# The opening of a decoder trunk: x loaded ahead on two queues, the norm chain ahead, and the first modulation columns as products on TensorE

## The chip, the cores and the metric

The kernel runs on one core of one Trainium2 chip, as one program. The metric is the device time of one execution in microseconds (us). Three runs of the kernel before gave 2087.95, 2089.53 and 2090.7 us, so the median is 2089.53 us. One more execution was taken with the hardware profiler on; all lines of the profile come from that one.

The engines of the core are TensorE (PE; its weight loads are listed as PEld), VectorE (DVE), ScalarE (ACT), GpSimd (POOL) and SyncE (SP). Each takes the instructions of its own queue in order. Transfers are issued by an engine's queue (here SP, and after the change ScalarE too) and run on 16 shared DMA engines.

## The reference, cut to what matters

Two layers, each of three sub-layers (SwiGLU FFN, token mixer, SwiGLU FFN), over 512 tokens of 1024 features. Every sub-layer starts with a normalised and modulated copy of x; its shift, scale and gate come from one conditioning vector c.

```
cond = silu(c)
mod = (cond @ ada_w[i] + ada_b[i]).reshape(bsz, 3, 3, D_MODEL)
shift, scl, gate = mod[:, :, 0], mod[:, :, 1], mod[:, :, 2]
h = rms_norm(x, norm_g[i, 0]) * (1 + scl[:, 0]) + shift[:, 0]
x = x + HALF * gate[:, 0] * swiglu(h, ffn_w_in[i, 0], ffn_w_out[i, 0])
```

rms_norm divides each token by the root of the mean square of its 1024 features. Nothing of the first FFN can be multiplied before the first slice of h is there, and for that the norm of x and the first scale and shift are needed.

## The kernel before, in words

x lies transposed in on-chip memory, as eight slices of 128 features by 512 tokens (`x[d]`, d from 0 to 7). All matmuls of the FFN run in three passes: each operand is split into a high part and a low part (`whi`, `wlo` for weights, `hhi`, `hlo` for h), and `mm3` (L167 to L170) multiplies high by high, high by low and low by high. ScalarE makes a high part (L164), VectorE the low part (L165).

The opening consists of these steps, and each step is traced in this order:

- The loads (L88 to L96), all on SP's queue: c broadcast to 128 partitions (`cond`, 512 KB), then the eight slices of x, with the small tables of norm gains and biases (`ngs`, `adabs`) after the fourth. ScalarE applies Silu to `cond` (L107).
- `Norm.start` (L251 to L269), the norm chain: ScalarE squares each slice (L254), VectorE adds the squares up (L256), TensorE sums over partitions with four one-column products (L260), VectorE computes the reciprocal root by integer trick and three Newton steps (L262, L195 to L203), VectorE scales the identity by it (`dg`, L267), and TensorE spreads it over all partitions with two products of 256 columns (L268).
- `ffn_first` (from L417) then walks over d. For each slice, `ada_first(d)` (L145) brings the scale and the shift of that slice: two tiles of 512 KB of modulation weights, each multiplied with `cond` and summed along the free axis. This is one VectorE instruction (L123), but the shift tile of an odd slice is multiplied on GpSimd (L120) and summed on ScalarE (L121). Three small VectorE instructions add the bias and the gain (L129, L130, L135). The tiles share a ring of four buffers (`ada`, L86), and SP issues their loads (L117).
- In the same step of d, for d below 6, one weight tile of the first FFN is loaded and split (`ffn_in`, `weights`, L172 to L180).
- `Norm.whole(d)` (L271 to L278): VectorE multiplies the slice with the norm (`xr`, L274), ScalarE applies scale and shift twice (`hhi` L275, `hf` L277), VectorE forms the low part (`hlo` L278).
- Last, TensorE multiplies what has become possible: with slice d, all weight tiles that are there. Six results (`hs`) grow side by side over the eight slices. Then the other tiles of the FFN (`gu`) follow.

The order of each engine's queue is not written by hand: a scheduler sorts the traced instructions by priority, which is the order of tracing unless a block says `tc.high_priority()`, and by the time at which it expects them to be ready.

Of the kernel before, what the change touches and what calls it, by code (L numbers as in the profile page):

```python
# [11 lines left out]
F32 = mybir.dt.float32  # L12
# [8 lines left out]
P = 128  # L21
# [20 lines left out]
NMOD = 24  # L42
NADA = 24
FIRST = 3
GC0 = math.sqrt(2.0 / math.pi)
GC1 = 0.044715
RSQ = float(0x5F3759DF)
# [1 line left out]


@with_exitstack
def decoder_kernel(ctx, tc, xT, cT, ng, adaw, adab, ffi, ffo, cwi, cw, cwo,
                   nwi, nwg, pos, w1, w2, qg, kg, nwo, rb, onehot, rowok, out):
    nc = tc.nc

# [29 lines left out]
    ada_es = ctx.enter_context(ExitStack())  # L85
    ap = ada_es.enter_context(tc.tile_pool(name="ada", bufs=4))  # L86
    cond = ap.tile([P, D], F32, name="cond", bufs=1)
    nc.sync.dma_start(cond, bass.AP(tensor=cT.tensor, offset=cT.offset, ap=[[0, P], [1, D]]))  # L88
    x = [cst.tile([P, T], F32, name=f"x{d}") for d in range(KD)]
    ngs = cst.tile([P, NSUB * KD], F32, name="ngs")  # L90
    adabs = cst.tile([P, NSUB * NMOD], F32, name="adabs")
    for d in range(KD):
        nc.sync.dma_start(x[d], xT[d])
        if d == 3:
            nc.sync.dma_start(ngs, ng)
            nc.sync.dma_start(adabs, adab)  # L96
    ident = cst.tile([P, P], F32, name="ident")
    make_identity(nc, ident)
    ones = cst.tile([P, P], F32, name="ones")
# [4 lines left out]
    rowm = cst.tile([P, 1], F32, name="rowm")  # L104
    mods = cst.tile([P, NSUB * NMOD], F32, name="mods")

    nc.scalar.activation(cond, cond, AF.Silu)  # L107

    def mod(s, kind, d):
        c = s * NMOD + kind * KD + d  # L110
# [1 line left out]

    def ada_tile(ap, s, t, split=False):
        raw = ap.tile([P, D], F32, name="adaraw")
        nc.sync.dma_start(raw, adaw[s * NADA + t])  # L117
        m = mods[:, s * NMOD + t:s * NMOD + t + 1]
        if split:
            nc.gpsimd.tensor_tensor(raw, raw, cond, ALU.mult)  # L120
            nc.scalar.activation(raw, raw, AF.Copy, accum_out=m)  # L121
        else:
            nc.vector.tensor_tensor_reduce(out=raw, in0=raw, in1=cond, scale=1.0, scalar=0.0,  # L123
                                           op0=ALU.mult, op1=ALU.add, accum_out=m)
# [12 lines left out]
    def ada_gate(s):  # L137
# [3 lines left out]
        else:  # L141
            nc.vector.tensor_add(mods[:, c:c + KD], mods[:, c:c + KD], adabs[:, c:c + KD])
            nc.vector.tensor_scalar(mods[:, c:c + KD], mods[:, c:c + KD], 0.5, None, op0=ALU.mult)

    def ada_first(ap, d):  # L145
        ada_tile(ap, 0, d)
        ada_tile(ap, 0, KD + d, d % 2 == 1)
        ada_scale(0, d, d + 1)
        ada_shift(0, d, d + 1)

    def ada_jobs(ap, s):
        lo = 2 * KD if s == 0 else 0
# [55 lines left out]
    class Norm:  # L208
# [40 lines left out]


        def start(self):  # L251
            for d in range(KD):
                dst = self.acc if d == 0 else tmp("sq", tag="sq")
                nc.scalar.activation(dst, x[d], AF.Square)  # L254
                if d:
                    nc.vector.tensor_tensor(self.acc, self.acc, dst, ALU.add)  # L256
            self.all = psum("pr", "pr")
            pv = psum("pr", "pr")
            for t in range(NB):
                nc.tensor.matmul(pv[:, t:t + 1], self.acc[:, t * P:(t + 1) * P], ones[:, 0:1], start=True, stop=True)  # L260
            v = sp.tile([P, NB], F32, name="nv", tag="nv", padded_shape=[P, NB])
            nc.vector.tensor_scalar(v, pv[:, 0:NB], 1.0 / D, EPS, op0=ALU.mult, op1=ALU.add)  # L262
            r = rsqrt(v, NB)
            for hf in range(2):
                dg = tmp("dg", HT, "dg").rearrange("p (a b) -> p a b", a=2)
                for t in range(2):
                    nc.vector.tensor_scalar(dg[:, t, :], ident, r[:, 2 * hf + t:2 * hf + t + 1], None, op0=ALU.mult)  # L267
                nc.tensor.matmul(self.all[:, hf * HT:(hf + 1) * HT], ones, dg.rearrange("p a b -> p (a b)"),  # L268
                                 start=True, stop=True)  # L269

        def whole(self, d):  # L271
            sc, sh = mod(self.s, 0, d), mod(self.s, 1, d)
# [141 lines left out]

    def ffn_first(s, f, nrm, nxt, extra, ahead, first, soon, own):  # L417
        with ExitStack() as es:
            hp = pool(es, "hp", 1)
            hid = Hidden(es, 18)  # L420
            h = nrm.alloc(hp)
            nj = FIRST
            early = spread(soon, PARTS[0][1] - nj)
            late = spread(extra, NJ - PARTS[0][1] + 2 * KD)

            def fill():
                early() if soon else late()

            js = [(j, c) for j in range(nj) for c in range(2)]
            w, os = [], [psum("hs") for _ in js]  # L430
            for d in range(KD):
                first(d)
                if d < len(js):
                    w.append(ffn_in(f, *js[d], own=own if d > 2 else None))
                nrm.whole(d)
                for n in range(len(w)):
                    for k in range(0 if n == d else d, d + 1):
                        project(os[n], w[n], 0, h, [(k, k)], k == 0, k == KD - 1)
            for j in range(nj):
                hid.activate(os[2 * j], os[2 * j + 1])  # L440
            for p, (j0, j1) in enumerate(PARTS):
                for j in range(max(j0, nj), j1):
                    hid.activate(*pair(f, j, h, own))
                    fill()
                n = j1 - j0
                a, ka = (hid.hi[j0:j1], hid.lo[j0:j1]), [(k, k) for k in range(n)]
                last = p == len(PARTS) - 1
                for d in range(KD - 3 if last else KD):
                    w = ffn_out(f, d, 1, j0, j1, own if d % 2 else None)
                    o = psum("y")  # L450
                    project(o, w, 0, a, ka, True, True)
                    if last:
                        residual(s, d, o, nxt)
# [664 lines left out]
    def ffn_ahead(f):  # L1118
# [2 lines left out]
    nxt = Norm(1)  # L1121
    soon = upto(1)
    w = ffn_first(0, 0, nrm, nxt, [small] + upto(2, NADA // 2), lambda: [weights(cwi[c], KD, P) for c in range(3)],
                  lambda d: ada_first(ap, d), soon, ap)
    nrm, nxt = nxt, Norm(2)
    w = conv(1, nrm, nxt, upto(6), w, ffn_ahead(1), ap)
    ada_es.close()
# [29 lines left out]
def _layout(v):  # L1157
    a = {k: np.asarray(t) for k, t in v.items()}
    r = {}
    r["xT"] = a["x"][0].T.reshape(KD, P, T)  # L1160
    r["cT"] = a["c"]
    r["ng"] = a["norm_g"].reshape(NSUB, KD, P).transpose(2, 0, 1).reshape(P, -1)

    cols = [(s * 3 + kind) * KD + d for s in range(3) for kind in (1, 0, 2) for d in range(KD)]
    aw = a["ada_w"].reshape(2, D, 3 * NMOD, P)[:, :, cols, :]
    r["adaw"] = aw.transpose(0, 2, 3, 1).reshape(2 * 3 * NMOD, P, D)
# [24 lines left out]
    return {k: np.ascontiguousarray(t) for k, t in r.items()}  # L1191
# [18 lines left out]
```

## Time and profile before

| | us |
|---|---|
| median of three runs | 2089.53 |
| the profiled execution, whole | 2082.89 |
| its span, from the first to the last instruction | 2081.1 |
| TensorE's first product of the first FFN (`hs`) | at 27.36 |
| first product after it (`gu`) | at 69.03 |
| TensorE busy in the span | 1985.5 |

A row of a timeline has the start in us from the span's start, the length in us, the engine, the line of the code, the operation, output and inputs by the program's names, shapes, and a count; in square brackets stands how long the engine had been idle and what ended the wait. SPq is SP's queue of transfers. A row of a group has, after the count, the busy time of the group in us, the mean of one instruction in ns, and the idle time before the group. Matmuls are pipelined, so a row's length is longer than the distance to the next row; distances between starts are used for rates.

### The profile page before, as it was taken

The numbers are of one execution on the slowest core, as the hardware profiler recorded it, in microseconds if no ns is written. First come the engines' busy times: TensorE is split into PE (matmuls) and PEld (weight loads), VectorE is DVE, ScalarE is ACT, GpSimd is POOL, SyncE is SP. The second block draws the span as 40 slices with busy tenths as digits, with TensorE's granted clock in tenths as the row PEclk, the third lists the DMA queues.
The fourth block names the chain that finished last, engine by engine and source line by source line (L and its number), as shares of the span: only waits on it lengthen the run. The fifth ranks groups of instructions, "written<-read, shape, count | busy, mean of one in ns | idle before, by whom it ended". The sixth has DMA issues, their size and how long they took to land.

```text
span 2081.1 us, 32232 instructions
## 1 busy us (share of the span) xinstructions
PE 1985.5 (95%) x12404; PEld 1769.8 (85%) x12404; DVE 1506.3 (72%) x2658; ACT 894.0 (43%) x1404; POOL 275.7 (13%) x395
## 2 busy tenths in 40 slices
PE   4999999999999999999999999988999989999999
PEld 3878888888888999888889989888788778898989
DVE  7878888664476677668767766784888868675855
ACT  4422223332254334335433433653767856343432
POOL 1000000100011111110111111000344530011100
PEclk9999999999999999999999999999999999999999
DMA  7888988322235556561455654223111133465642
GB/s 270 309 303 318 331 310 317 141 96 77 91 97 126 153 142 166 147 173 42 131 145 145 164 142 147 84 92 100 41 38 43 36 97 91 121 165 160 159 118 82
DMA packets 110662, 307.38 MB, mean 148 GB/s; under 512 B 14923, under 2 KB 15307, under 8 KB 110508
## 3 DMA queue, kind: packets, MB, share of 16 engines
q1 hardware_dynamic: 89532, 260.48, 37.1%
q0 software_dynamic: 20976, 44.84, 11.2%
q8 instruction: 97, 1.59, 0.3%
q14 instruction: 57, 0.47, 0.1%
HBM read 302.12 MB, written 3.15 MB: 147 GB/s over the span
## 4 chain that ended last, share of the span: by engine, by line
PE 38%; DVE 7%; ACT 4%; issue 2%; DMA 1%; POOL 0%; DVEq 0%; ACTq 0%; POOLq 0%; SPq 0%
PE gu L168 6%; PE gu L169 6%; PE gu L170 6%; PE y L168 4%; PE y L169 4%; PE y L170 4%; ACT whi L164 1%; DVE wlo L165 1%; DVE L L942 1%; PE nat L168 1%; PE nat L170 1%; PE nat L169 1%; PE s L932 1%; DVE ptl L977 1%; PE ty L170 1%
## 5 line engine op out<-in xcount | busy, mean ns | idle before, releaser
L164 ACT ACTIVATE whi<-wraw 128x1024 fp32r<-128x1024 f32 (+2 forms) x296 | 295.3, 1001 | 589.8 <-PE y L169 237.9
L165 DVE TENSOR_TENSOR wlo<-wraw,whi 128x1024 fp32r<-128x1024 f32 (+2 forms) x296 | 340.4, 1152 | 85.2 <-ACT whi L164 82.7
L168 PE MATMUL gu<-hhi,whi 128*128 128x256 f32 (+1 forms) x808 | 266.8, 330 | 2.0 <-ACT whi L164 2.0
L169 PE MATMUL gu<-hlo,whi 128*128 128x256 f32 (+1 forms) x808 | 266.5, 330 | 0.0
L170 PE MATMUL gu<-hhi,wlo 128*128 128x256 f32 (+1 forms) x808 | 266.1, 329 | 0.0
L168 PE MATMUL y<-ahi,whi 128*128 128x512 f32 x611 | 241.8, 399 | 3.5 <-ACT ahi L164 3.5
L169 PE MATMUL y<-alo,whi 128*128 128x512 f32 x611 | 244.4, 400 | 0.0
L170 PE MATMUL y<-ahi,wlo 128*128 128x512 f32 x611 | 241.2, 395 | 0.0
L487 POOL DMA_DIRECT2D qa<-in_ffi x114 | 103.8, 991 | 650.3 <-DMA qa<-in_ffi 335.4
L123 DVE CUSTOM_DVE_ANT_0 adaraw<-adaraw,cond 128x1024 f32<-128x1024 f32 x140 | 169.2, 1221 | 21.0 <-DMA adaraw<-in_adaw 20.0
L168 PEld LDWEIGHTS gu<-hhi,whi 128*128 128x128 f32 x808 | 152.2, 188 | 19.1 <-ACT whi L164 3.9
L169 PEld LDWEIGHTS gu<-hlo,whi 128*128 128x128 f32 x808 | 151.8, 188 | 15.5
L170 PEld LDWEIGHTS gu<-hhi,wlo 128*128 128x128 f32 x808 | 152.1, 188 | 14.9
L164 ACT ACTIVATE qbh<-qb 128x1536 fp32r<-128x1536 f32 x57 | 84.9, 1490 | 164.7 <-PE gu L169 143.5
L168 PEld LDWEIGHTS y<-ahi,whi 128*128 128x128 f32 x611 | 114.7, 189 | 36.3 <-ACT ahi L164 7.8
L554 DVE SCALAR_TENSOR_TENSOR x<-y,mods,x 128x512 f32<-128x512 f32 x72 | 54.1, 751 | 120.5 <-PE y L170 120.5
L168 PE MATMUL gu<-th,qah 128*128 128x256 f32 x456 | 131.0, 287 | 9.2 <-ACT p L512 9.2
L170 PEld LDWEIGHTS y<-ahi,wlo 128*128 128x128 f32 x611 | 115.5, 189 | 27.6
L169 PEld LDWEIGHTS y<-alo,whi 128*128 128x128 f32 x611 | 115.6, 189 | 26.3 <-DVE alo L165 0.3
L170 PE MATMUL gu<-th,qal 128*128 128x256 f32 x456 | 130.8, 287 | 0.0
L169 PE MATMUL gu<-tl,qah 128*128 128x256 f32 x456 | 130.5, 286 | 0.0
L168 PE MATMUL gu<-th,qbh 128*128 128x256 f32 x456 | 129.4, 284 | 0.0
(280 smaller groups left out, 5168.0 us busy)
## 6 DMA issues: line engine op xcount, KB each, us to landing
adaraw<-in_adaw SPq DMA_DIRECT2D x144, 512.0 KB, 5.5
wraw<-in_ffi SPq DMA_DIRECT2D x119, 512.0 KB, 4.3
qa<-in_ffi SPq DMA_DIRECT2D x114, 256.0 KB, 4.1
qa<-in_ffi POOLq DMA_DIRECT2D x114, 256.0 KB, 5.4
wraw<-in_ffo SPq DMA_DIRECT2D x72, 384.0 KB, 4.1
qb<-in_ffi POOLq DMA_DIRECT2D x57, 256.0 KB, 3.3
wraw<-in_cwi SPq DMA_DIRECT2D x24, 512.0 KB, 3.3
wraw<-in_ffo SPq DMA_DIRECT2D x20, 512.0 KB, 4.6
```

Source lines behind the costliest of these rows:

```text
L123: nc.vector.tensor_tensor_reduce(out=raw, in0=raw, in1=cond, scale=1.0, scalar=0.0, op0=ALU.mult, op1=ALU.add, accum_out=m)
L164: nc.scalar.activation(hi, src, AF.Copy)
L165: nc.vector.tensor_tensor(lo, src, hi, ALU.subtract)
L168: nc.tensor.matmul(o, sh, mh, start=first, stop=False)
L169: nc.tensor.matmul(o, sh, ml, start=False, stop=False)
L170: nc.tensor.matmul(o, sl, mh, start=False, stop=last)
L487: nc.gpsimd.dma_start(qa[:, i], quart(1, 0), accum_op=ALU.add)
L554: nc.vector.scalar_tensor_tensor(x[d], o, mod(s, 2, d), x[d], op0=ALU.mult, op1=ALU.add)
L932: nc.tensor.matmul(sps[:, off:off + n], Q[q][:, i * P:(i + 1) * P], m[:, 0:n], start=(e == 0), stop=(e == 1))
L942: nc.vector.tensor_tensor_reduce(out=Ls[u][:, LOFF[i]:LOFF[i] + n], in0=sps[:, off:off + n], in1=tb[:, q, T - n:T], scale=1.0, scalar=3e38 ...
L977: return lambda: nc.vector.tensor_tensor(lo, pt[:, 0:off], hi, ALU.subtract)
```

## The change

- x is loaded ahead of everything else. The even slices are issued by SP, the odd ones by ScalarE. After them SP loads c once more in another layout (`conk`, 128 partitions by 8, 4 KB), then `adabs` and `ngs`. The broadcast `cond` is loaded and passed through Silu after the modulation tiles of the first three slices.
- `Norm.start` is traced with high priority. Its sum and its spread share one PSUM buffer, and the four `dg` pieces lie in one buffer, so that both products of L268 follow them.
- A new function, `ada_columns`, makes scale and shift of slices 0, 1 and 2 (`NKM` = 3). For each it loads two tiles of 512 KB in another layout (`adak`: the same weights with the contraction on the partitions) into the same ring of four buffers, and multiplies each on TensorE in eight one-column products that accumulate into one column of PSUM. Three VectorE instructions then add bias and gain for all three slices at once.
- For slices 3 to 7 `ada_first` does what it did, but always on VectorE: the branch with GpSimd and ScalarE (L119 to L121) is gone.
- The host lays out the two new arrays, `ck` and `adak`.

```diff
-    nc.sync.dma_start(cond, bass.AP(tensor=cT.tensor, offset=cT.offset, ap=[[0, P], [1, D]]))
+    conk = ap.tile([P, KD], F32, name="conk", bufs=1)
     for d in range(KD):
-        nc.sync.dma_start(x[d], xT[d])
-        if d == 3:
-            nc.sync.dma_start(ngs, ng)
-            nc.sync.dma_start(adabs, adab)
+        (nc.scalar if d % 2 else nc.sync).dma_start(x[d], xT[d])
+    nc.sync.dma_start(conk, ck)
+    nc.sync.dma_start(adabs, adab)
+    nc.sync.dma_start(ngs, ng)
...
-    nc.scalar.activation(cond, cond, AF.Silu)
+    nc.scalar.activation(conk, conk, AF.Silu)
...
-        if split:
-            nc.gpsimd.tensor_tensor(raw, raw, cond, ALU.mult)
-            nc.scalar.activation(raw, raw, AF.Copy, accum_out=m)
-        else:
-            nc.vector.tensor_tensor_reduce(out=raw, in0=raw, in1=cond, scale=1.0, scalar=0.0,
-                                           op0=ALU.mult, op1=ALU.add, accum_out=m)
+        nc.vector.tensor_tensor_reduce(out=raw, in0=raw, in1=cond, scale=1.0, scalar=0.0,
+                                       op0=ALU.mult, op1=ALU.add, accum_out=m)
...
+    def ada_columns(ap, n):
+        po = psum("pr", "pr")
+        for d in range(n):
+            for c in range(2):
+                raw = ap.tile([P, D], F32, name="adaraw")
+                nc.sync.dma_start(raw, adak[2 * d + c])
+                o = po[:, c * KD + d:c * KD + d + 1]
+                for k in range(KD):
+                    nc.tensor.matmul(o, raw[:, k * P:(k + 1) * P], conk[:, k:k + 1], start=(k == 0), stop=(k == KD - 1))
+        nc.vector.tensor_add(mods[:, 0:n], po[:, 0:n], adabs[:, 0:n])
+        nc.vector.scalar_tensor_tensor(mods[:, 0:n], mods[:, 0:n], 1.0, ngs[:, 0:n], op0=ALU.add, op1=ALU.mult)
+        nc.vector.tensor_add(mods[:, KD:KD + n], po[:, KD:KD + n], adabs[:, KD:KD + n])
+        nc.sync.dma_start(cond, bass.AP(tensor=cT.tensor, offset=cT.offset, ap=[[0, P], [1, D]]))
+        nc.scalar.activation(cond, cond, AF.Silu)
+
     def ada_first(ap, d):
-        ada_tile(ap, 0, d)
-        ada_tile(ap, 0, KD + d, d % 2 == 1)
-        ada_scale(0, d, d + 1)
-        ada_shift(0, d, d + 1)
+        if d >= NKM:
+            ada_tile(ap, 0, d)
+            ada_tile(ap, 0, KD + d)
+            ada_scale(0, d, d + 1)
+            ada_shift(0, d, d + 1)
...
-            self.all = psum("pr", "pr")
-            pv = psum("pr", "pr")
...
+            pv = self.all = psum("pr", "pr")
+            with tc.high_priority():
...
+                dg = tmp("dg").rearrange("p (a b) -> p a b", a=NB)
+                for t in range(NB):
+                    nc.vector.tensor_scalar(dg[:, t, :], ident, r[:, t:t + 1], None, op0=ALU.mult)
+                for hf in range(2):
+                    nc.tensor.matmul(self.all[:, hf * HT:(hf + 1) * HT], ones,
+                                     dg[:, 2 * hf:2 * hf + 2].rearrange("p a b -> p (a b)"), start=True, stop=True)
...
             w, os = [], [psum("hs") for _ in js]
+            columns()
             for d in range(KD):
                 first(d)
```

More of the change, by code (lines that the diff above doesn't have):

```diff
@@ L44 @@
 FIRST = 3
+NKM = 3
 GC0 = math.sqrt(2.0 / math.pi)
@@ L51, in decoder_kernel @@
 @with_exitstack
-def decoder_kernel(ctx, tc, xT, cT, ng, adaw, adab, ffi, ffo, cwi, cw, cwo,
+def decoder_kernel(ctx, tc, xT, cT, ck, ng, adak, adaw, adab, ffi, ffo, cwi, cw, cwo,
                    nwi, nwg, pos, w1, w2, qg, kg, nwo, rb, onehot, rowok, out):
@@ L111, in mod, with ada_tile @@
         return mods[:, c:c + 1]
-    def ada_tile(ap, s, t, split=False):
+    def ada_tile(ap, s, t):
         raw = ap.tile([P, D], F32, name="adaraw")
@@ L251, in start @@
         def start(self):
[L252 to L256, printed above, removed]
-            self.all = psum("pr", "pr")
-            pv = psum("pr", "pr")
[L259 to L269, printed above, removed]
+            pv = self.all = psum("pr", "pr")
+            with tc.high_priority():
+                for d in range(KD):
+                    dst = self.acc if d == 0 else tmp("sq", tag="sq")
+                    nc.scalar.activation(dst, x[d], AF.Square)
+                    if d:
+                        nc.vector.tensor_tensor(self.acc, self.acc, dst, ALU.add)
+                for t in range(NB):
+                    nc.tensor.matmul(pv[:, t:t + 1], self.acc[:, t * P:(t + 1) * P], ones[:, 0:1], start=True, stop=True)
+                v = sp.tile([P, NB], F32, name="nv", tag="nv", padded_shape=[P, NB])
+                nc.vector.tensor_scalar(v, pv[:, 0:NB], 1.0 / D, EPS, op0=ALU.mult, op1=ALU.add)
+                r = rsqrt(v, NB)
+                dg = tmp("dg").rearrange("p (a b) -> p a b", a=NB)
+                for t in range(NB):
+                    nc.vector.tensor_scalar(dg[:, t, :], ident, r[:, t:t + 1], None, op0=ALU.mult)
+                for hf in range(2):
+                    nc.tensor.matmul(self.all[:, hf * HT:(hf + 1) * HT], ones,
+                                     dg[:, 2 * hf:2 * hf + 2].rearrange("p a b -> p (a b)"), start=True, stop=True)
         def whole(self, d):
@@ L413, in pair, with ffn_first @@
         return gu
-    def ffn_first(s, f, nrm, nxt, extra, ahead, first, soon, own):
+    def ffn_first(s, f, nrm, nxt, extra, ahead, columns, first, soon, own):
         with ExitStack() as es:
@@ L1123, in decoder_kernel @@
     w = ffn_first(0, 0, nrm, nxt, [small] + upto(2, NADA // 2), lambda: [weights(cwi[c], KD, P) for c in range(3)],
-                  lambda d: ada_first(ap, d), soon, ap)
+                  lambda: ada_columns(ap, NKM), lambda d: ada_first(ap, d), soon, ap)
     nrm, nxt = nxt, Norm(2)
@@ L1161, in _layout @@
     r["cT"] = a["c"]
+    r["ck"] = a["c"][0].reshape(KD, P).T
     r["ng"] = a["norm_g"].reshape(NSUB, KD, P).transpose(2, 0, 1).reshape(P, -1)
@@ L1165, in _layout @@
     aw = a["ada_w"].reshape(2, D, 3 * NMOD, P)[:, :, cols, :]
+    r["adak"] = aw[0].reshape(KD, P, 3 * NMOD, P)[:, :, [d + c for d in range(NKM) for c in (0, KD)], :] \
+        .transpose(2, 1, 0, 3).reshape(2 * NKM, P, D)
     r["adaw"] = aw.transpose(0, 2, 3, 1).reshape(2 * 3 * NMOD, P, D)
```

## The prediction

> **What bounds the kernel now.** I read the page's head first, then busy time by stage, then TensorE's instructions in order of time.
>
> ```profile
> span 2081.1 us, 32232 instructions
> ```
> ```profile
> 0.00:12.77 12.77, 0.00 (x1) 0.01 (x1) 5.28 (x9) 7.17 (x10) 0.70 (x6) 1.00 0.88 307
> 12.77:27.36 14.59, 4.31 (x13) 2.79 (x13) 11.29 (x31) 4.02 (x6) 2.35 (x1) 1.00 0.77 293
> 27.36:47.49 20.13, 15.14 (x51) 10.00 (x52) 20.13 (x32) 9.96 (x14) 5.97 (x2) 1.00 0.74 248
> 47.49:65.00 17.51, 17.51 (x76) 14.33 (x77) 15.15 (x31) 8.25 (x12) 3.34 (x1) 1.00 0.91 339
> 65.00:120.00 55.00, 55.00 (x241) 44.79 (x240) 44.27 (x67) 22.72 (x30) 0.00 (x0) 1.00 0.79 287
> 120.00:400.00 280.00, 280.00 (x1226) 226.73 (x1225) 225.72 (x345) 73.91 (x91) 6.30 (x4) 0.99 0.83 299
> ```
>
> The columns are stage and length, then busy time of TensorE, its weight load, VectorE, ScalarE and GpSimd, granted clock, DMA share and GB/s. From 47.49 to 400 us TensorE has no idle time. So whatever time the opening gains or loses before its matmul stream ends goes through to the end, one for one; VectorE (44.27 of 55) and DMA (0.79) have room there. The opening is read in TensorE's order of time (start, length, line):
>
> ```profile
> 12.77 1.87 PE L260 MATMUL pr<-ones,nacc 128*128 128x1 f32 x8 [12.77 <-DVE nacc L256]
> 21.83 1.22 PE L268 MATMUL pr<-dg,ones 128*128 128x256 f32 x2 [7.20 <-DVE dg L267]
> 24.50 1.22 PE L268 MATMUL pr<-dg,ones 128*128 128x256 f32 x2 [1.45 <-DVE dg L267]
> 27.36 1.22 PE L168 MATMUL hs<-hhi,whi 128*128 128x512 f32 x2 [1.63 <-ACT hhi L275]
> 29.93 0.63 PE L168 MATMUL hs<-hhi,whi 128*128 128x512 f32 x1
> 30.36 0.63 PE L169 MATMUL hs<-hlo,whi 128*128 128x512 f32 x1
> ...
> 33.40 0.40 PE L169 MATMUL hs<-hlo,whi 128*128 128x512 f32 x1
> 33.63 0.40 PE L170 MATMUL hs<-hhi,wlo 128*128 128x512 f32 x1
> ...
> 47.49 1.43 PE L168 MATMUL hs<-hhi,whi 128*128 128x512 f32 x5 [1.70 <-ACT hhi L275]
> ...
> 60.01 0.39 PE L168 MATMUL hs<-hhi,whi 128*128 128x512 f32 x1
> 68.34 0.39 PE L168 MATMUL hs<-hhi,whi 128*128 128x512 f32 x1
> 69.03 0.39 PE L168 MATMUL gu<-hhi,whi 128*128 128x512 f32 x1
> ```
>
> The opening's product (`hs`: eight slices, six weight tiles, three matmuls each, 144 in all) runs from T0 = 27.36 to 69.03. From 60.01 to 68.34 lie 36 matmuls, 0.231 us each; 144 of them need 33.3 us. So 8.4 us of the 41.7 are waits and a slow clock: 29.93 to 30.36 is 0.43 per matmul of the same form, about twice the 0.23 of 33.40 to 33.63, though the clock column says 1.00 throughout. At the start of a run I read the clock from spacing.
>
> **The change: what it takes away.** cond's 512 KB no longer lies ahead of x and of the first modulation tile.
>
> ```profile
> 0.74 0.38 SPq L88 DMA_DIRECT2D cond<-in_cT  x1
> 7.18 1.06 SPq L117 DMA_DIRECT2D adaraw<-in_adaw  x2
> 8.29 0.43 SPq L178 DMA_DIRECT2D wraw<-in_ffi  x1
> ```
> ```profile
> DMA to landing us min/median/max: 5.0/5.3/5.5
> ```
> ```profile
> 10.00:15.00 5.00, 1.87 (x8) 1.78 (x8) 2.73 (x6) 1.79 (x4) 0.00 (x0) 1.00 1.03 413
> ```
>
> The second row's first tile lands 5.0 to 5.5 later, at 12.2 to 12.7. 512 KB at 413 GB/s are 1.3 us; at the slower early rate of 307 GB/s 1.7. So the first column tile lands, and the sum of squares (12.77) ends, near 10.6 to 11.2; with x's issue on two queues I take 10.6 for both (bounds 9.0 and 11.4). ScalarE's four issues (0.38 each by cond's row) come before x lands, so they are hidden.
>
> The norm chain is no longer broken by GpSimd and by the modulation:
>
> ```profile
> 14.67 0.16 DVE L262 TENSOR_SCALAR nv<-pr 128x4 f32<-128x4 f32 x1 [1.96 <-PE pr L260]
> ...
> 17.52 2.29 DVE L202 TENSOR_TENSOR rs_b<-rs_a,nv 128x4 f32<-128x4 f32 x1
> 20.23 0.16 DVE L202 TENSOR_TENSOR rs_b<-rs_a,nv 128x4 f32<-128x4 f32 x1
> 21.02 0.16 DVE L203 SCALAR_TENSOR_TENSOR rs_r<-rs_b,rs_r 128x4 f32<-128x4 f32 x1
> ```
> ```profile
> 17.44 2.35 POOL L120 TENSOR_TENSOR adaraw<-adaraw,cond 128x1024 f32<-128x1024 f32 x1 [16.13 <-DMA adaraw<-in_adaw]
> ```
>
> The same 4-column multiply takes 2.29 us while GpSimd multiplies and 0.16 otherwise. Undisturbed the steps follow each other by 0.2 (20.23 to 21.02 is four), so 12 of them take 2.4, the four `dg` about 1.0: 3.4 instead of 9.8 (14.67 to 24.5). That gain counts only if nothing else is late. Something is.
>
> **What it adds.** Six tiles times eight products, two passes each (the norm's four products are x8), make 96 passes of one column on TensorE. The nearest row is 12.77: 1.87 for eight, 0.23, or 0.213 from start to start. On a fast clock:
>
> ```profile
> 596.20 0.50 PE L240 MATMUL pr<-ones,nacc 128*128 128x1 f32 x4
> 596.56 0.60 PE L168 MATMUL hs<-hhi,whi 128*128 128x256 f32 x3
> ...
> 601.89 0.59 PE L248 MATMUL pr<-dg,ones 128*128 128x256 f32 x2
> ```
>
> four passes in 0.36, 0.09 each. So the columns cost 8.6 to 20.5 us (22 by busy time), by the clock. Which one? The nearest thing to a long run of narrow products is in attention:
>
> ```profile
> L887 PE MATMUL pc<-kch,q 128*128 128x32 f32 x16 | 3.6, 262 | 0.2 <-DVE q L872 0.2
> ```
> ```profile
> 1461.30:1464.70 3.40, 3.40 (x32) 3.40 (x33) 1.11 (x4) 1.20 (x3) 2.28 (x5) 1.00 0.02 5
> 1464.70:1468.10 3.40, 3.40 (x18) 3.40 (x18) 1.81 (x7) 1.80 (x7) 0.00 (x0) 0.50 0.00 0
> ```
>
> For 3.4 us TensorE and its weight load were full of 32-column matmuls (x16 here, x16 with kcl), and the next 3.4 us had clock 0.50. Products of 32 columns did not hold a fast clock; one column will hardly win one. I take 0.213: 20.5 us.
>
> The Trainium skill (TensorE: Matmul & The Clock Gate, Part 1) says that about 3.4 us of sustained activity release the clock. By that rule, read as any activity, the columns would be fast after their first 4 us: the fast-clock rival below. The pair of rows above speaks against that reading.
>
> TensorE runs its queue in order. From 10.6 it has 1.87 (L260), 2.44 (two rows of L268) and 20.5: 24.8, so the last column ends at 35.4. This assumes that part of the columns stands between L260 and L268, so that TensorE does not idle during the 3.4 of rsqrt. All six must be there before the three adds (0.6, steps of 0.2); from there the way is that of slice 0 now:
>
> ```profile
> 26.49 0.81 ACT L275 ACTIVATE hhi<-xr,mods 128x512 fp32r<-128x512 f32 x1 [4.57 <-DVE xr L274]
> ```
>
> 0.9 from 26.49 to the first `hs` matmul at 27.36. **T0 = 36.9**, 9.5 later than now.
>
> Other new waits are covered by this. The tile ring has four buffers, so columns 5 and 6 are issued when TensorE has finished tiles 1 and 2 (about 16 and 20; they land by 25 even at 5 us each). Behind them on SP's queue stand cond, the first three weight tiles and the tiles of slice 3; the first weight, issued at 8.3 now, goes at about 20 and is split by 27, hidden only because T0 is 36.9. At T0 = 25 this would be the bound.
>
> **After T0** the stream is fed better. Slices 0 to 2 (27 matmuls) come at once. Slices 3 to 5 each cost VectorE:
>
> ```profile
> L123 DVE CUSTOM_DVE_ANT_0 adaraw<-adaraw,cond 128x1024 f32<-128x1024 f32 x15 | 18.1, 1216 | 0.0
> L165 DVE TENSOR_TENSOR wlo<-wraw,whi 128x1024 fp32r<-128x1024 f32 x7 | 8.5, 1215 | 0.0
> L274 DVE TENSOR_TENSOR xr<-x,pr 128x512 f32<-128x512 f32 x8 | 5.4, 680 | 1.1 <-PE pr L268 1.1
> ```
>
> two of L123, one L165, two of 0.68, and 0.5 of small adds: 5.5, against 21, 27 and 33 matmuls (4.9, 6.2, 7.6); slices 6 and 7 4.3 against 4.2. Beside this VectorE loses six L123 of slices 0 to 2 to TensorE (five; GpSimd did one) and takes three odd ones from GpSimd; its stalls under GpSimd (2.1 above, three more alike) go. So TensorE bounds the stream: 33.3, plus a slow clock for the first 5 us at half rate, 2.5 (it now ends between 30.36 and 33.40, 3 to 6 us after T0: bounds 1.5 and 3.0), plus 0.7 for the wait on the first low part, one VectorE step of L274's size. The stream ends at 36.9 + 33.3 + 2.5 + 0.7 = **73.4**, 4.4 later than 69.03. Its waits shrink from 8.4 to 3.2, a gain of 5.2; T0 loses 9.5.
>
> The profiled execution took 2082.89 (span 2081.1 and 1.8 around it); it gives 2087.3. The median of the runs shown is 6.6 higher, 2089.53; I add 4.4 to that: **2093.9**. Measurement can tell about 0.2% from no change, 4.2 us: the forecast stands on that edge. With starts of 9.0 to 11.4 and the clock's bounds the case reaches from +2 to +6.5, 2091.5 to 2096.
>
> **Rivals.**
> Norm first: if the product L268 stands ahead of all columns in TensorE's queue, TensorE idles 3.4 in the chain and T0 is 40.3, end 76.8: +7.8, 2097.3. For it: the chain gets priority everywhere. Against: at 596.56 other matmuls stand between L240 and that chain's second product (L248, 601.89), though it has priority too.
> Fast clock, the faster side: if one-column passes raise the clock, the first 4 us are slow, the rest 0.09; buffers then bound (tile 6 lands near 21.5, columns end 23.5), T0 25. The stream needs 33.3 and some 2.5 of waits for DMA and VectorE: end 61, -8, 2081.5. Faster begins where T0 is under 32.5 (69.03 less 36.5), so where the columns end before 31. For it: no row shows a one-column run of over 1.9 us.
> Columns partly covered: tiles land near 9 and the clock is fast for a third of the passes (32 at 0.09 save 3.9), which brings T0 to 31 to 34: -1.5 to +1.5, 2089.5.
>
> **How the numbers follow.** Main case 0.56, norm first 0.20, fast clock 0.17, partly covered 0.07. The range must reach to the fast clock to leave out no more than 2 in 10: 2081 to 2099. The main case's own range is 2091.5 to 2096. Slower by over 0.2%: half of the main case and norm first, 0.48; same 0.32 (the other half and most of the last case); faster 0.20.
>
> **What would show it.** TensorE's 96 passes 0.213 apart (or 0.09); the first `hs` matmul near 37; its spacing 0.43 for some 5 us, then 0.231 without waits; the first `gu` near 73. L202 at 0.16 throughout. Wrong if the columns stand 0.1 apart, if T0 is under 33, or if slices 3 to 7 wait for VectorE.

## The result, and the profile after

The changed kernel took 2094.83 us (median of 17 runs) beside 2085.89 us for the kernel before (17 runs): a ratio of 1.0041, 95% interval 1.0029 to 1.0053. That is 8.6 us more (6.0 to 11.1). The forecast was 4.4 more; the sign and the range held, the size was half of it, and 8.6 lies above the main case's own +2 to +6.5 (only the interval reaches into it). That the forecast time of 2093.9 comes within 1 us of the measured one is luck: it was added to 2089.53, the median of three runs, and the median of all 17 is 3.6 lower.

TensorE's instructions of the opening, in order of time, are the answer to the rows of before (start, length, line, in brackets the idle time ahead and what ended it). The change shifted the lines: L272 is the old L256, L274 the old L260, L282 the old L268, L178 the split of a weight, L182 to L184 the three passes, L151 the columns.

```profile
14.12 1.87 PE L274 MATMUL pr<-ones,nacc 128*128 128x1 f32 x8 [14.12 <-DVE nacc L272]
15.84 13.79 PE L151 MATMUL pr<-conk,adaraw 128*128 128x1 f32 x64
29.50 2.05 PE L282 MATMUL pr<-dg,ones 128*128 128x256 f32 x4
31.34 6.83 PE L151 MATMUL pr<-conk,adaraw 128*128 128x1 f32 x32
42.77 0.80 PE L182 MATMUL hs<-hhi,whi 128*128 128x512 f32 x1 [4.60 <-ACT whi L178]
...
45.01 0.63 PE L184 MATMUL hs<-hhi,wlo 128*128 128x512 f32 x1
45.44 0.63 PE L182 MATMUL hs<-hhi,whi 128*128 128x512 f32 x1
...
50.06 0.39 PE L184 MATMUL hs<-hhi,wlo 128*128 128x512 f32 x1
50.29 0.39 PE L183 MATMUL hs<-hlo,whi 128*128 128x512 f32 x1
...
78.66 0.39 PE L182 MATMUL gu<-hhi,whi 128*128 128x512 f32 x1
```

From 14.12 to 38.17 TensorE has no gap: product, 64 passes, spread, 32 passes. Then it stands for 4.60 us, and what ends that is ScalarE's split of a weight. The first `gu` comes at 78.66, 9.6 later than the 69.03 of before. The last two stretches by busy time (columns as in the prediction):

```profile
38.17:42.77 4.60, 0.00 (x1) 0.01 (x1) 2.27 (x7) 4.17 (x6) 0.00 (x0) 1.00 0.63 229
42.77:78.66 35.89, 35.46 (x145) 28.59 (x146) 31.39 (x60) 17.85 (x23) 0.00 (x0) 1.00 0.71 265
```

In the last stretch TensorE is busy for 35.46 of 35.89: the stream is fed. ScalarE worked 4.17 of the 4.60 in which TensorE stood, so it had a queue to get through. Its rows:

```profile
5.74 0.63 ACT L270 ACTIVATE sq<-x 128x512 f32<-128x512 f32 x1 [0.19 <-DMA x<-in_xT]
6.39 1.28 ACT L108 ACT_TABLE_LOAD   x1
9.42 0.21 ACT L108 ACTIVATE conk<-conk 128x8 f32<-128x8 f32 x1 [1.75 <-DMA conk<-in_ck]
...
38.60 0.81 ACT L289 ACTIVATE hhi<-xr,mods 128x512 fp32r<-128x512 f32 x1 [25.47 <-DVE mods L153]
39.32 0.80 ACT L291 ACTIVATE hf<-xr,mods 128x512 f32<-128x512 f32 x1
40.02 1.04 ACT L156 ACTIVATE cond<-cond 128x1024 f32<-128x1024 f32 x1
40.97 0.80 ACT L289 ACTIVATE hhi<-xr,mods 128x512 fp32r<-128x512 f32 x1
41.67 1.04 ACT L178 ACTIVATE whi<-wraw 128x1024 fp32r<-128x1024 f32 x1
```

Two things stand here. The small Silu of `conk` lies between the third and the fourth square, and ScalarE waits there from 6.37 to 9.42 for a table load and then for `conk` itself. And the first weight's split is fifth in the queue behind slice 0's two halves, the Silu of `cond` and a half of slice 1; before all of these ScalarE was idle for 25.47. SP's queue shows when the two loads went out:

```profile
4.57 0.33 SPq L95 DMA_DIRECT2D conk<-in_ck  x1
...
23.70 1.38 SPq L192 DMA_DIRECT2D wraw<-in_ffi  x3
```

`conk`, the ninth transfer, is issued at 4.57, although SP had issued its fourth slice by 2.54. The first weight goes out at 23.70 and waits in memory for most of the time up to 41.67.

### The profile page after: what moved, and what is told of

Read it like the earlier page. It is cut to its first block, busy times and chain, and to the rows that moved or that the text cites. A ratio compares the mean times of both kernels' runs of the same rounds, so it can differ in the third digit from the quotient of the medians.

```text
span 2092.6 us, 32410 instructions
## 1 busy us (share of the span) xinstructions
PE 2005.5 (96%) x12500; PEld 1797.4 (86%) x12500; DVE 1494.8 (71%) x2648; ACT 890.6 (43%) x1398; POOL 264.4 (13%) x391
## 3 DMA queue, kind: packets, MB, share of 16 engines
q0 software_dynamic: 20976, 44.84, 11.2%
q10 hardware_dynamic: 576, 1.05, 0.1%
## 4 chain that ended last, share of the span: by engine, by line
PE 38%; DVE 7%; ACT 4%; issue 2%; DMA 2%; POOL 0%; DVEq 0%; ACTq 0%; POOLq 0%; SPq 0%
PE gu L182 6%; PE gu L183 6%; PE gu L184 6%; PE y L182 4%; PE y L184 4%; PE y L183 4%; ACT whi L178 1%; DMA qa<-in_ffi 1%; DVE L L957 1%; DVE wlo L179 1%; PE nat L182 1%; PE nat L184 1%; PE nat L183 1%; PE ty L182 1%; PE ty L183 1%
## 5 line engine op out<-in xcount | busy, mean ns | idle before, releaser
L178 ACT ACTIVATE whi<-wraw 128x1024 fp32r<-128x1024 f32 (+2 forms) x296 | 295.1, 1001 | 557.5 <-PE y L183 245.8
L182 PE MATMUL gu<-hhi,whi 128*128 128x256 f32 (+1 forms) x808 | 265.8, 329 | 2.0 <-ACT whi L178 2.0
L184 PE MATMUL gu<-hhi,wlo 128*128 128x256 f32 (+1 forms) x808 | 264.9, 328 | 0.0
L182 PE MATMUL y<-ahi,whi 128*128 128x512 f32 x611 | 241.4, 398 | 6.2 <-ACT ahi L178 6.2
L184 PE MATMUL y<-ahi,wlo 128*128 128x512 f32 x611 | 243.8, 399 | 0.0
L120 DVE CUSTOM_DVE_ANT_0 adaraw<-adaraw,cond 128x1024 f32<-128x1024 f32 x138 | 166.9, 1222 | 38.3 <-DMA adaraw<-in_adaw 36.5
L182 PEld LDWEIGHTS gu<-hhi,whi 128*128 128x128 f32 x808 | 152.2, 188 | 18.1 <-ACT whi L178 3.9
L184 PEld LDWEIGHTS gu<-hhi,wlo 128*128 128x128 f32 x808 | 152.1, 188 | 13.8
L178 ACT ACTIVATE qbh<-qb 128x1536 fp32r<-128x1536 f32 x57 | 84.9, 1490 | 165.6 <-PE gu L183 144.2
L182 PEld LDWEIGHTS y<-ahi,whi 128*128 128x128 f32 x611 | 114.7, 189 | 38.2 <-ACT ahi L178 11.4
L184 PEld LDWEIGHTS y<-ahi,wlo 128*128 128x128 f32 x611 | 115.6, 189 | 27.2
L182 PE MATMUL gu<-th,qah 128*128 128x256 f32 x456 | 129.8, 285 | 7.0 <-ACT p L527 7.0
L184 PE MATMUL gu<-th,qal 128*128 128x256 f32 x456 | 129.6, 284 | 0.0
L182 PE MATMUL gu<-th,qbh 128*128 128x256 f32 x456 | 129.0, 283 | 0.0
```

Of the source, the lines that this page charges most:

```text
L178: nc.scalar.activation(hi, src, AF.Copy)
L182: nc.tensor.matmul(o, sh, mh, start=first, stop=False)
L184: nc.tensor.matmul(o, sl, mh, start=False, stop=last)
```

## The experiments

Theory: the opening decides, one for one; the columns cost 0.213 us a pass because the clock is slow, and what the forecast missed are two places in ScalarE's order, at the start (3.5) and ahead of the first weight (3.1). Rivals: one-column passes cost 0.213 at any clock; the late loads set the start whatever ScalarE does; VectorE takes whatever TensorE and ScalarE give back. Each experiment goes by its name in the table. All twelve were timed beside the kernel before; "opening" is the first `gu` less 69.03, from the one profiled execution of each.

| kernel | norm's product | first `hs` | first `gu` | opening | ratio to before (95%) |
|---|---|---|---|---|---|
| before | 12.77 | 27.36 | 69.03 | 0 | 1 |
| after | 14.12 | 42.77 | 78.66 | +9.6 | 1.0041 (1.0029 to 1.0053) |
| conk_first | 13.48 | 42.13 | 78.03 | +9.0 | 1.0050 (1.0034 to 1.0066) |
| start | 11.54 | 40.19 | 76.08 | +7.1 | 1.0043 (1.0024 to 1.0063) |
| whi | 13.96 | 39.31 | 76.09 | +7.1 | 1.0024 (1.0012 to 1.0035) |
| both | 11.00 | 36.35 | 73.07 | +4.0 | 1.0014 (1.0002 to 1.0026) |
| cols_warm | 13.82 | 35.72 | 70.87 | +1.8 | 0.9986 (0.9974 to 0.9999) |
| both_warm | 15.27 | 46.42 | 82.7 | +13.7 | 1.0031 (1.0018 to 1.0045) |
| nkm0 | 17.50 | 31.67 | 66.66 | -2.4 | 0.9992 (0.9979 to 1.0005) |
| nkm1 | 13.81 | 28.96 | 68.92 | -0.1 | 0.9979 (0.9963 to 0.9996) |
| rest_only | 18.07 | 32.24 | 68.46 | -0.6 | 0.9976 (0.9964 to 0.9989) |
| pool_only | 13.08 | 25.53 | 63.49 | -5.5 | 0.9977 (0.9963 to 0.9991) |
| nkm1_both | 11.52 | 24.89 | 63.48 | -5.5 | 0.9946 (0.9927 to 0.9966) |
| nkm1_chain | 11.38 | 25.10 | 62.62 | -6.4 | 0.9947 (0.9930 to 0.9963) |

### The price of a pass: cols_warm

```diff
+    wide = ap.tile([P, T], mybir.dt.bfloat16, name="wide", bufs=1)
+    nc.vector.memset(wide, 1.0)
...
+        with tc.high_priority():
+            for _ in range(45):
+                nc.tensor.matmul(bank, wide[:, 0:P], wide, start=True, stop=True)
...
+                    if k % 3 < 2:
+                        nc.tensor.matmul(bank, wide[:, 0:P], wide, start=True, stop=True)
```

Unused 512-column products stand ahead of the norm's product and among the columns.

> The changed kernel with wide bf16 products of a constant on TensorE, whose result is never used: 45 of 512 columns while TensorE has nothing to do, and 32 among the 48 column products. Theory (the clock, not the engine, makes the columns dear): with wide products the clock is fast from before the first column, so a column pass takes 0.10 to 0.11 instead of 0.213: 96 passes 10 us, the 32 wide ones add 7, the whole run of columns takes 17 instead of 20.6, and the stream's first matmuls come 0.23 apart instead of 0.43, which saves 2 to 3 more. First gu near 72 to 74, 5 to 6 us faster than the changed kernel in spite of the added work. Rival (one-column passes cost 0.213 whatever the clock, for the weight load): the run of columns takes 27 us and the time rises by 4 to 7 us.

TensorE in order of time:

```profile
1.46 10.83 PE L149 MATMUL hs<-wide 128*128 128x512 bf16 x39 [1.46 <-DVE wide L99]
13.82 1.05 PE L281 MATMUL pr<-ones,nacc 128*128 128x1 f32 x8 [1.53 <-DVE nacc L279]
14.73 1.73 PE L156 MATMUL pr<-conk,adaraw 128*128 128x1 f32 x14
...
16.99 1.01 PE L149 MATMUL hs<-wide 128*128 128x512 bf16 x2
...
32.19 0.95 PE L156 MATMUL pr<-conk,adaraw 128*128 128x1 f32 x8
```

The same eight passes of the norm take 1.05 after wide products and 1.87 without them; eight column passes take 0.95, where they took 1.7 (8 of 0.213). In the middle (16.99) even the wide products take about 0.4 each, where the six in a row at 19.56 stand 0.23 apart. The busy time of this stretch and of the next one shows why in its clock column, 0.73 and then 1.00:

```profile
14.70:21.00 6.30, 6.30 (x35) 4.58 (x35) 2.83 (x16) 1.06 (x1) 0.00 (x0) 0.73 0.47 166
22.20:34.30 12.10, 12.10 (x105) 11.15 (x103) 2.92 (x3) 1.95 (x2) 0.00 (x0) 1.00 0.72 263
```

TensorE had waited 1.53 us ahead of the norm's product; then came 22 one-column passes in a row (8 of the norm, 14 of the columns), and near 16.3 the clock went. With wide products between the passes, and some in a row, it came back. Whether the wait or the narrow passes took it away, this run does not separate. But 0.213 is the price at the slow clock and about 0.11 at the fast one: that rival falls. The first `gu` comes 7.8 earlier than in the changed kernel although TensorE does 81 products more (45 ahead, 36 among the columns); part of that is that another queue order also splits the weights early here. Time: 0.9986.

### The two places in ScalarE's queue: conk_first, start, whi, both

conk_first loads `conk` and passes it through Silu ahead of x:

```diff
+    nc.sync.dma_start(conk, ck)
+    with tc.high_priority():
+        nc.scalar.activation(conk, conk, AF.Silu)
     for d in range(KD):
         (nc.scalar if d % 2 else nc.sync).dma_start(x[d], xT[d])
```

> The changed kernel with one thing moved: the small load of c (conk) and its Silu stand ahead of x, so ScalarE's squares no longer wait for it. Theory (columns in series on a slow clock, and three waits around them): in the changed kernel ScalarE stands from 6.37 to 9.42 us for a second table load and for conk, so the sum of squares ends at 14.1 instead of about 11. Without it the columns start near 11, the first hs product comes near 40 instead of 42.77, the first gu near 75.6 instead of 78.66: 3 us faster than the changed kernel, still some 5 us slower than the kernel before. Rival (the late sum of squares is covered, the columns wait for their tiles): first gu stays within 0.5 us of 78.66.

It missed: the norm's product came 0.6 earlier, no more. ScalarE, whose queue issues the odd slices:

```profile
6.62 0.35 ACTq L97 DMA_DIRECT2D x<-in_xT  x1
...
12.07 0.63 ACT L270 ACTIVATE sq<-x 128x512 f32<-128x512 f32 x1 [1.84 <-DMA x<-in_xT]
```

Now the last slice of x is the ninth transfer: it is issued at 6.62 by ScalarE, which had begun its squares by then, and is late. One wait had taken the place of the other, so this run told nothing of the term. start leaves the loads as they are and ties the Silu to the last square:

```diff
-    nc.scalar.activation(conk, conk, AF.Silu)
...
+        nc.scalar.activation(conk, conk, AF.Silu)
         po = psum("pr", "pr")
...
+                nc.vector.scalar_tensor_tensor(conk, dst[:, 0:KD], 0.0, conk, op0=ALU.mult, op1=ALU.add)
                 for t in range(NB):
```

> Edit: the Silu of the small condition tile stands behind the eight squares on ScalarE (tied to the last square by adding zero times that square to the tile). Theory, the start term was mis-sized because ScalarE stood between third and fourth square: the norm's product starts near 10.6 instead of 14.12, the first hs matmul near 39.3 instead of 42.77, the first gu near 75.2 instead of 78.66, and the time is 3.5 under that of the changed kernel. Rival, the late loads set the start whatever ScalarE does: the product starts at 13.5 or later, as when the tile was loaded ahead of x, and the time falls by under 1.

The opening shrank by 2.58, as far as the norm's product moved (14.12 to 11.54), where 3.5 was expected. The time did not show it: 2.58 is 0.12%, and the interval is 0.2% to either side. whi instead ties the columns' adds to the first weight's split, so that the split stands ahead of slice 0:

```diff
+        whi = early()
+        nc.vector.scalar_tensor_tensor(adabs[:, 0:1], whi[:, 0, 0:1], 0.0, adabs[:, 0:1], op0=ALU.mult, op1=ALU.add)
         nc.vector.tensor_add(mods[:, 0:n], po[:, 0:n], adabs[:, 0:n])
...
+            def w0():
+                w.append(ffn_in(f, *js[0]))
+                return w[0][0]
...
-            columns()
+            columns(w0)
...
-                if d < len(js):
+                if 0 < d < len(js):
```

> Edit: the split of the first weight tile stands ahead of slice 0 on ScalarE (the adds of the columns are tied to it by adding zero times the split's result to one bias column). Theory, ScalarE's queue order cost 3.1 between the last column and the first hs matmul: that gap falls from 4.6 to about 1.5, the first hs matmul comes near 39.7, the first gu near 75.6, the time is 3.1 under that of the changed kernel. Rival, the next thing late takes the gain (the low part of the weight, the Silu of cond, the second weight tile): waits of 2 to 3 stand inside the stream and the first gu stays above 77.5.

```profile
27.26 1.06 ACT L180 ACTIVATE whi<-wraw 128x1024 fp32r<-128x1024 f32 x1 [14.28 <-DMA wraw<-in_ffi]
30.35 1.06 ACT L158 ACTIVATE cond<-cond 128x1024 f32<-128x1024 f32 x1 [2.03 <-DMA cond<-in_cT]
38.45 0.81 ACT L291 ACTIVATE hhi<-xr,mods 128x512 fp32r<-128x512 f32 x1 [7.04 <-DVE mods L155]
```

The split now runs at 27.26, when its tile lands: the 27 that the prediction had written. TensorE waits 1.29 for slice 0 instead of 4.60. The first `gu` gains 2.57; 0.9 of the wait comes back in the stream. Both edits together:

> Edit: both of the above. Theory, the two terms are all that the forecast missed: product near 10.6, first hs near 36.2, first gu near 72.1, time 6.6 under that of the changed kernel, so 2 over the kernel before. Rival, they share a cause or another wait comes up (column tiles 5 and 6, the first weight's load): the gain is under 5.

```profile
11.00 1.87 PE L276 MATMUL pr<-ones,nacc 128*128 128x1 f32 x8 [11.00 <-DVE nacc L273]
...
36.35 0.79 PE L183 MATMUL hs<-hhi,whi 128*128 128x512 f32 x1 [1.30 <-ACT hhi L291]
...
73.07 0.39 PE L183 MATMUL gu<-hhi,whi 128*128 128x512 f32 x1
```

These are the forecast's own milestones: 11.00 (10.6), 36.35 (36.9), 73.07 (73.4). The ratio 1.0014 (1.0002 to 1.0026) is 2.9 us over the kernel before, 0.4 to 5.4, where the forecast had 4.4. The two gains add up: 5.6, beside 2.6 and 2.6 alone (the product came 0.5 earlier here than in start).

### Keeping the clock: both_warm

As both, with 28 wide products first and a 256-column product of the tile itself after every four one-column products:

```diff
+            for _ in range(28):
+                nc.tensor.matmul(bank, wide[:, 0:P], wide, start=True, stop=True)
...
+                    if k % 4 == 3:
+                        nc.tensor.matmul(bank[:, 0:HT], ones, raw[:, 0:HT], start=True, stop=True)
```

> Edit: both of the above, and 28 unused 512-column products ahead of the norm and one unused 256-column product after every four one-column products, which keep TensorE wide and its clock high. Theory, the columns' price is the clock's: passes 0.09 to 0.11 apart, columns end near 28 instead of 33, first hs near 29.5, stream of 36 to 38, first gu 66 to 68, time 1 to 3 under the kernel before. Rival, the stream then waits for VectorE and the modulation tiles of slices 3 to 7 as with one slice of columns (40.0 long): first gu near 69.5, time equal to the kernel before.

```profile
10.53 1.10 PE L157 MATMUL hs<-adaraw,ones 128*128 128x256 f32 x4 [0.23 <-DMA adaraw<-in_adak]
13.50 1.97 PE L157 MATMUL hs<-adaraw,ones 128*128 128x256 f32 x4 [1.87 <-DMA adaraw<-in_adak]
15.27 1.70 PE L283 MATMUL pr<-ones,nacc 128*128 128x1 f32 x8
16.83 8.67 PE L155 MATMUL pr<-conk,adaraw 128*128 128x1 f32 x40
```

It missed. The four 256-column passes took 1.10 at 10.53 and 1.97 at 13.50: the clock went while TensorE waited 1.87 for the second tile, with no one-column pass before it. The 40 passes then ran 0.213 apart, and here the granted clock says so: 0.50 from 17.00 to 25.50. The wider products among the later passes did not bring the clock back (0.50 up to 46.00), and only cost their own time. How wide and how dense the products must be was not measured.

### Fewer columns, and the parts alone: nkm1, nkm0, rest_only, pool_only

nkm1 is the changed kernel with `NKM = 1`, nkm0 with 0 (no columns, no `conk`, no `adak`; `cond` still behind x).

> The changed kernel with one slice's columns on TensorE instead of three (32 passes instead of 96); slices 1 and 2 go to VectorE as slices 3 to 7 do. Theory: 64 passes at 0.213 us leave TensorE's series, 13.7 us, and the first weight's split is no longer behind slice 1 on ScalarE: first hs product near 26 to 28 instead of 42.77. The stream then waits for VectorE again, some 5 us in all: first gu near 63 to 67, 11 to 15 us faster than the changed kernel and 2 to 6 faster than the kernel before. Rival (the opening is bounded by loads and VectorE, the columns are hidden): first gu at 75 or later.

> The changed kernel without any column on TensorE: x ahead on two queues, norm chain with priority, no GpSimd part; all eight slices' scale and shift on VectorE. conk and the second layout of the weights are left out, cond is loaded right after x. Theory: this keeps the parts that gain and drops the one that loses. First hs product near 22 to 25, first gu near 61 to 66: 13 to 17 us faster than the changed kernel, 3 to 8 faster than the kernel before. Rival (the columns pay for themselves, the loss lies in the order of the queues): no more than 3 us faster than the changed kernel.

Both missed their first `gu`: nkm1 has 68.92 where 63 to 67 was expected, nkm0 66.66 for 61 to 66. One slice of columns instead of three brings the first `hs` from 42.77 to 28.96, and the stream then grows from 35.9 to 40.0 us. ScalarE waits there for VectorE at each slice, for instance:

```profile
32.92 0.81 ACT L289 ACTIVATE hhi<-xr,mods 128x512 fp32r<-128x512 f32 x1 [2.37 <-DVE xr L288]
```

In nkm0 the Silu of `cond` stands between the squares and waits there for its 512 KB until 11.66, so the norm's product starts at 17.50. rest_only loads `cond` ahead of x again and keeps the rest of the change (priority, two queues, one bank, no GpSimd):

> The change without its columns and with cond's load ahead of x as before: x on two queues, the norm chain ahead in all queues, one bank, no GpSimd part; all eight slices' modulation on VectorE. Theory, the columns are the only part that costs: first hs matmul at 25 to 28, stream 36 to 38, first gu 62 to 66 (69.03 in the kernel before), time 3 to 6 under the kernel before. Rival, VectorE becomes the bound, with 16 modulation tiles of 1.22 ahead of and between the slices: slices wait 2 or more each for VectorE, first gu at 68 or later, time equal to before.

The norm's product is late here too (18.07), and the chain is broken again, now by VectorE's own modulation tiles and splits:

```profile
19.97 0.16 DVE L264 TENSOR_SCALAR nv<-pr 128x4 f32<-128x4 f32 x1 [0.75 <-PE pr L262]
20.05 1.22 DVE L120 CUSTOM_DVE_ANT_0 adaraw<-adaraw,cond 128x1024 f32<-128x1024 f32 x1
...
27.52 0.87 DVE L268 TENSOR_SCALAR dg<-ident,rs_r 128x128 f32<-128x128 f32 x4
```

From 19.97 to 27.52, for steps that take 2.4 undisturbed: the priority did not keep the queue clear. By its opening the rival is nearer (68.46), by its time the theory (0.9976); it decides nothing between them. pool_only is the kernel before with one edit:

```diff
-        ada_tile(ap, 0, KD + d, d % 2 == 1)
+        ada_tile(ap, 0, KD + d)
```

> The kernel before without the GpSimd part alone: its four multiplies go to VectorE, nothing else changes. Theory of the prediction, GpSimd's multiply stretches the norm chain: no step of 2.29 is left in the rsqrt, the first hs matmul comes 2 to 4 earlier than 27.36, first gu 66 to 69. Rival, four more VectorE tiles of 1.22 each take back what the chain gains: first gu at 69 or later, time equal or over the kernel before.

This is the largest gain in the opening of a single part: first `gu` at 63.49, beyond the expected 66 to 69, time 0.9977. What TensorE waited for in the stream, before and here (total, times, longest):

```profile
PE hs L168 <- ACT hhi L275: 3.7, 3, 1.7
PE hs L169 <- DVE hlo L278: 2.1, 3, 1.3
PE hs L170 <- DVE wlo L165: 0.7, 1, 0.7
```

```profile
PE hs L168 <- ACT hhi L275: 2.0, 2, 1.6
PE hs L168 <- ACT whi L164: 0.9, 2, 0.7
PE hs L169 <- DVE hlo L278: 0.5, 1, 0.5
```

3.1 us of waits go (6.5 to 3.4, the wait ahead of T0 not counted) and T0 comes 1.8 earlier (2 to 4 was expected), although VectorE does four multiplies more. In the kernel before these two VectorE steps lie under GpSimd's multiplies (29.54 to 32.23 and 42.69 to 45.98):

```profile
29.92 2.85 DVE L278 TENSOR_TENSOR hlo<-hf,hhi 128x512 fp32r<-128x512 f32 x1
...
43.65 2.35 DVE L130 SCALAR_TENSOR_TENSOR mods<-mods,ngs 128x1 f32<-128x1 f32 x1
```

They take 0.69 and 0.15 in pool_only. What GpSimd took off VectorE it gave back in stretched steps. They need not be all of the gain: the edit also takes off ScalarE the four sums of 1.04 to 1.06 that followed GpSimd's multiplies, and no run parts the two.

### A version that beats both: nkm1_both, nkm1_chain

nkm1_both is both with `NKM = 1`.

> Columns for one slice alone, with the Silu behind the squares and the first weight's split ahead of slice 0. Theory, start and queue order cost here what they cost with three slices: the norm's product near 10.8, first hs near 24, and the stream's waits for VectorE move ahead with it: first gu near 65 to 66 (68.92 without the two), time 6 under the kernel before. Rival, VectorE's work bounds the stream whatever its start: first gu 68 or later, time as with one slice alone, 4 under the kernel before.

It has the first `gu` at 63.48 (65 to 66 was expected) and the time at 0.9946 (0.9927 to 0.9966), the best of all. In its chain VectorE still stands for a weight and for the columns:

```profile
16.27 1.23 DVE L180 TENSOR_TENSOR wlo<-wraw,whi 128x1024 fp32r<-128x1024 f32 x1 [1.10 <-ACT whi L179]
...
20.25 0.16 DVE L153 TENSOR_TENSOR mods<-pr,adabs 128x1 f32<-128x1 f32 x1 [2.47 <-PE pr L150]
```

nkm1_chain ties the columns' adds to the last diagonal tile:

```diff
+                nc.vector.scalar_tensor_tensor(adabs[:, 0:1], dg[:, 3, 0:1], 0.0, adabs[:, 0:1], op0=ALU.mult, op1=ALU.add)
                 for hf in range(2):
```

> As the one-slice version with both mends, and the columns' adds on VectorE stand behind the norm chain (tied to its last diagonal tile by zero times it), so that VectorE does not wait for TensorE's columns inside the chain (2.47 there). Theory, VectorE's queue is what bounds the stream now, so its wait goes to the end one for one: diagonal tiles near 18.3 instead of 20.64, first gu near 61 instead of 63.48, opening 8 under the kernel before. Rival, TensorE's columns and the loads set the first slice anyway and VectorE waits elsewhere: first gu at 63 or later. As to the whole time: if the one-slice version's 0.5% came from the opening, this one is again 0.3 to 0.6% under the kernel before; if part of it was chance, the ratio falls back to what the opening gives, 0.996 to 0.997.

```profile
17.10 0.87 DVE L282 TENSOR_SCALAR dg<-ident,rs_r 128x128 f32<-128x128 f32 x4
...
22.02 0.69 DVE L291 TENSOR_TENSOR xr<-x,pr 128x512 f32<-128x512 f32 x1 [2.84 <-PE pr L285]
```

The diagonal tiles came 3.5 earlier, and VectorE then stood 2.84 for the spread, which TensorE runs behind the columns (L285 at 19.93): the wait moved, and the first `gu` gained 0.9, to 62.62, nearer to the rival's 63 than to the expected 61. The ratio 0.9947 (0.9930 to 0.9963) says that the 0.5% was no chance. The opening explains 5.5 and 6.4 of the 11.2 and 11.1 us (0.54% and 0.53% of the 2080 and 2086 that the kernel before took beside them); where the other 5 come from was not found.

## Why the prediction was right and wrong

**Right for this change: the opening decides.** The opening grows by 9.6, and the time by 8.6 (6.0 to 11.1). From the first `gu` on, the one profiled execution of each needs 2012.1 before and 2013.9 after. **Right: the columns' price.** 96 passes 0.213 apart; the run from the norm's product to the last column took 24.05, where 24.8 was written, and TensorE's queue had the assumed order: columns, spread, columns, so "norm first" did not come about. **Right: the stream.** 35.89 for 36.5, with 0.43 per matmul for about 5 us, then 0.227. L216 (the old L202) took 0.16 throughout.

**Wrong: "I take 10.6 for both (bounds 9.0 and 11.4)".** The sum of squares ended at 14.12, 3.5 later and outside the bounds. The step counted ScalarE's four issues as hidden and left out the one thing that the change puts into ScalarE's queue: the small Silu, with a table load of 1.28, behind a load that goes out ninth. The runs start and both, with that Silu behind the squares, have the product at 11.54 and 11.00: 2.6 to 3.1 of the 3.5. The 0.4 to 0.9 that is left was not traced. The Trainium skill (ScalarE: Activation LUTs, What ACT_TABLE_LOAD costs) gives some 1.28 for the load and 2.66 for a switch with its drain; the load agrees (1.28), but in the run both the Silu starts 1.30 after the load begins, so no run here shows the drain.

**Wrong: "the first weight ... is split by 27, hidden only because T0 is 36.9".** The tile was there by 27 (whi), but ScalarE's queue had it behind four other operations, at 41.67. The gap from the last column to the first `hs` was 4.6 instead of 1.5. The prediction asked when the tile lands and not where its split stands in the queue.

So 73.4 and 78.66 differ by +3.5 (start), -0.75 (TensorE's run), +3.1 (gap), -0.6 (stream). The run both, with the two mended, gave 73.07.

**The fast-clock rival** was wrongly put in one respect: the columns do not raise the clock, but 512-column products beside them did (cols_warm); one of 256 columns after every four did not (both_warm). The Trainium skill's rule (TensorE: Matmul & The Clock Gate, Part 1), read as any activity, failed here: in 24 us of unbroken work, 104 one-column passes and four of 256 columns, the columns stayed at 0.213, and the clock rose at 48.42, 5.7 us after the 512-column products began and 4.0 after the last gap among them.

**Under-valued: the GpSimd part.** The prediction saw the steps of 2.29, and summed this gain with the columns' loss. pool_only shows that the part alone is worth 5.5 of the opening. nkm0 and rest_only do not show it, because there the Silu of `cond` and VectorE's tiles break the chain anew. The wait for VectorE that would have sunk the forecast did not come with three slices of columns; it came with one.

**Open.** One for one does not hold for every run. In six of the twelve experiments (cols_warm, both_warm, nkm1, rest_only, nkm1_both, nkm1_chain) the opening lies outside the interval of the time, and each time the kernel is faster than its opening says: both_warm has +13.7 in the opening and +6.5 (3.8 to 9.4) in time, nkm1 -0.1 and -4.4 (0.8 to 7.7 faster). From the first `gu` to the end of the span the profiled executions need between 2000.8 (nkm1_both) and 2026.4 (start), 2012.1 before; but each is one execution, that of start the slowest of its ten. So the time after the opening moves by several us too. One place is visible: between 100 and 425 us TensorE waits in the FFN's second product in the changed kernel,

```profile
PE y L182 <- ACT ahi L178: 2.7, 2, 2.4
PE y L183 <- DVE alo L179: 0.9, 2, 0.4
```

and in the same stretch neither before nor both has a wait of `y`. The order of the queues there depends on what the opening leaves behind; that this explains the rest was not tested.

## What to carry to other kernels

For each instruction that a change adds, however small, write down whose queue it stands in and what stands behind it; ask of a moved load not only when it lands but which instruction consumes it and where that stands. Before an engine is relieved by moving work to a fresh one, try what happens when the helper is just taken away: here the one-line removal was worth more than the whole change. A product of one column costs by the clock, and it does not earn the fast clock itself.

## What the runs showed of the hardware

- One-column f32 passes: 0.213 from start to start in all 96 of the changed kernel, with no gap among them, 0.10 to 0.12 in cols_warm beside enough 512-column products. The clock column shows a drop that follows a fast stretch (0.73 in cols_warm from 14.70 to 21.00, 0.50 in both_warm from 17.00 to 46.00, with the same 0.213), but says 1.00 for the slow columns of the changed kernel, ahead of which TensorE had not been fast; there only the spacing shows the clock.
- Moving one Silu between squares costs a second table load of 1.28; ScalarE then waits in order for the Silu's input with five squares behind it.
- In the changed kernel and in conk_first the first eight transfers were issued without a pause, and the ninth went out late: `conk` at 4.57 in the changed kernel, where SP's queue stood 2.0 until a slice of x had landed, and the last slice of x at 6.62 in conk_first, where squares stood in the same queue. What sets the limit was not tested.
- A 128x1 VectorE step took 2.35 under a GpSimd multiply and 0.15 without it; a 128x512 step 2.85 and 0.69.
